# A long convolution's transforms as plain fp32 matmuls of the tiles themselves, in place of three fp32r matmuls of high and low parts

## Chip, core and metric

The kernel runs on one NeuronCore of a Trainium2 chip. The metric is the device time of one execution in microseconds (us), smaller is better. Engines have these names here: PE (TensorE, matmuls), DVE (VectorE), ACT (ScalarE), POOL (GpSimd) and SP (SyncE, which here only issues DMAs; "SPq" is its queue).

## The reference, cut to what matters

The reference is a two-layer diffusion backbone. The second layer's mixer runs a Hyena operator beside differential attention; the change touches only the Hyena operator's two long convolutions, which the reference writes with an FFT:

```
def bidir_fft_conv(u, h_fwd, h_bwd):
    L, C = h_fwd.shape
    k = jnp.concatenate([h_fwd, jnp.zeros((1, C), h_fwd.dtype), h_bwd[1:][::-1]], axis=0)
    uf = jnp.fft.rfft(u.astype(jnp.float32), n=2 * L, axis=1)
    kf = jnp.fft.rfft(k, n=2 * L, axis=0)
    y = jnp.fft.irfft(uf * kf[None], n=2 * L, axis=1)[:, :L]
...
        z = v
        for o, gate in enumerate((x1, x2)):
            z = gate * (bidir_fft_conv(z, h[:, o, 0], h[:, o, 1]) + z * hy_bias[o])
```

Here L is 1024 and C is 512. Everything is float32.

## The kernel before, in words

`hy_conv` holds the two convolutions ("orders", `o` = 0 and 1). The FFT is a matmul with matrices of cosines and sines that come from DRAM. The 1024 rows are taken as four residues `r` (in the order `RS` = 0, 2, 1, 3), a tile `hz` of 128 x 2 x 512 each. For one residue `forward` makes four sums, `fa_ps` (two halves `kt` of the frequencies, `c` = real and imaginary), each the sum of two products of a 128x128 matrix with a 128x512 tile. `take` folds the sums of two residues into tiles `hw` on DVE. When all four residues are there, `spectrum` multiplies by the filter's spectrum `hk`, on DVE alone, `kt` = 0 and then `kt` = 1: 16 operations on 128x1024 and 16 on 128x512 for each `kt`. It leaves one tile for each residue, two in `ht` and two in `hw`. `backward` then makes two sums `y_ps` for each residue, each of four products (two with the tiles of `kt` = 0, two with those of `kt` = 1), and DVE multiplies the sum by the gate, which stands in `hz`. So each order has 32 products forward and 32 backward, 128 in all.

A product is not one matmul. `split` (L91 to L95) makes of each tile a high part in fp32r (a copy on ACT) and a low part (tile minus high part, on DVE), the matrices come from DRAM in two parts already, and `mm3` (L98 to L105) makes three matmuls of each product: high with high (L103), and the two mixed ones (L104, L105). Each is 128x128 with 128x512, in fp32r. The tiles `hz_hi`, `hz_lo` are the parts of `hz`, `hbhi`, `hblo` those of `ht` and `hw`.

The order of the stages around it is this:
- Order 0's forward transforms run among the last steps of the attention (`weave`: scores `s_ps`, transposes `pt_ps`, and the product with the values `o_ps`, L2244, which is one plain fp32 matmul of 128x128 with 128x512; the trace has two records for each).
- Order 0's spectrum runs while the attention ends.
- Order 0's backward and order 1's forward transforms follow each other residue by residue. I call this stretch the middle stage.
- Order 1's spectrum, with the out-projection of the attention's half (`ho_t` transposes, `ho_ps` matmuls by `mm3`, 192 of them) beside it on PE. The generator `proj_half` is advanced by a count, `due += 0.33` for each of the spectrum's steps.
- Order 1's backward transforms, the store of `hy`, and then the MLP's first part, which reads `hy` back (`y_in`) and starts with `op_ps`.

The engines run their instructions in the order of the program text that the scheduler leaves, one queue for each engine. POOL issues the loads of the matrices (`hm`, L1993) and also makes the low parts `wo_lo` of the out-projection's weights, so a load can stand behind a `wo_lo`. SP issues the loads of `hz`, `hk`, `wo_raw` and others.

Of the kernel before, what the change touches and what calls it, by code (L numbers as in the profile page):

```python
# [8 lines left out]
F32 = mybir.dt.float32  # L9
FR = mybir.dt.float32r  # L10
# [1934 lines left out]
def hy_conv(g, pool):  # L1945
# [1 line left out]

    nc = g.nc
    g.hy = g.dram.tile([1024, HY], F32, name="hy")
    RS = (0, 2, 1, 3)
# [35 lines left out]
    def load_mat():  # L1989
        if todo:  # L1990
            src, i, j = todo.pop(0)
            m = pool.tile([128, 2, 2, 2, 128], FR, name="hm", bufs=3)
            nc.gpsimd.dma_start(out=m.rearrange("p a b w k -> p (a b w k)"), in_=g.i[src][i, j])  # L1993
            mats.append(m)

    def matrix():
# [1 line left out]
        return mats.pop(0)  # L1998

    def load_z(j, r):  # L2000
        z = tile2("hz", 2)
        nc.sync.dma_start(out=z, in_=rows(g.hv[j], r))
        return z

    def parts(z, name, bufs):
        hi, lo = (tile2(name + x, bufs, FR) for x in ("hi", "lo"))
        split(g, hi, lo, z)
        return hi, lo

    def forward(r, z, A):  # L2010

        hi, lo = z

        def take(kt, c, ps):
            a = A[kt]
            if r < 2:
                if c == 0:
                    a["d", r] = tile2("hw", 8)
                nc.scalar.copy(a["d", r][:, c], ps)
                return  # L2020
            i = r - 2
            if c == 0:
                a["s", i] = tile2("hw", 8)
            d = a["d", i][:, c]
            add(a["s", i][:, c], ps, d)
            nc.vector.scalar_tensor_tensor(d, ps, -1.0, d, op0=ALU.mult, op1=ALU.add)

        for kt in range(2):
            m = matrix()
            for c in range(2):  # L2030
                ps = psa(g, [128, HY], name="fa_ps", tag="hy")
                mm3(g, ps, [(m[:, c, j, 0], m[:, c, j, 1], hi[:, j], lo[:, j]) for j in range(2)])
                flush()
                later.append(lambda kt=kt, c=c, ps=ps: take(kt, c, ps))
                yield 1
# [59 lines left out]
    def backward(o, r, A, made):  # L2095

        z = load_z(1 + o, r)
        bs = [parts(A[kt][r], "hb", 3) for kt in range(2)]
        yield 1

        def take(jt, ps):
            mul(z[:, jt], ps, z[:, jt])
# [7 lines left out]
        for jt in range(2):  # L2110
            m = matrix()
            ps = psa(g, [128, HY], name="y_ps", tag="hy")
            mm3(g, ps, [(m[:, kt, c, 0], m[:, kt, c, 1], bs[kt][0][:, c], bs[kt][1][:, c])
                        for kt in range(2) for c in range(2)])
            flush()
            later.append(lambda jt=jt, ps=ps: take(jt, ps))
            yield 1
# [1 line left out]
    for _ in range(2):  # L2119
        load_mat()  # L2120
    A = [{}, {}]
    zs = [load_z(0, r) for r in RS[:2]]
    for i, r in enumerate(RS):
        z = parts(zs[i], "hz_", 1)
        if i + 2 < 4:
            zs.append(load_z(0, RS[i + 2]))
        yield 1
        yield from forward(r, z, A)
    flush()
    for o in range(2):  # L2130
        for kt in range(2):
# [2 lines left out]
        for i, r in enumerate(RS):  # L2134
            yield from backward(o, r, A, zs)
            if o == 0:
                if z:
                    yield from forward(RS[i - 1], z, nxt)
                flush()
                z = parts(zs.pop(r), "hz_", 1)  # L2140
        flush()
        if o == 0:
            yield 1
# [250 lines left out]
def tile_kernel(ctx, tc, ins, out):  # L2394
# [93 lines left out]
    with ExitStack() as st:  # L2488
# [14 lines left out]
        with tc.tile_pool(name="ho1", bufs=1, reuse_waits="tile") as pool:  # L2503
# [5 lines left out]
            for n, kind in enumerate(hyena):  # L2509
                if n % 16 == 8:  # L2510
                    next(rest, None)
                due += 0.33 if kind == 2 else 0.0
                if due >= 1.0:
                    next(half, None)
                    due -= 1.0
# [20 lines left out]
def _consts():  # L2536
# [42 lines left out]

    r, kt, p, im, jt, k = np.ix_(*(np.arange(n) for n in (4, 2, 128, 2, 2, 128)))  # L2580
    m = turns(kt * 128 + k, 4 * (jt * 128 + p) + r, im)
    c["k_df"] = np.ascontiguousarray(parts(m)).reshape(4, 2, 128, 1024)

    r, jt, k, kt, im, p = np.ix_(*(np.arange(n) for n in (4, 2, 128, 2, 2, 128)))
    m = turns(kt * 128 + k, 4 * (jt * 128 + p) + r, im) / 1024
    c["k_di"] = np.ascontiguousarray(parts(m)).reshape(4, 2, 128, 1024)

    im, b, kt, x, p, s, k = np.ix_(*(np.arange(n) for n in (2, 2, 2, 2, 128, 4, 128)))
    m = turns(kt * 128 + k + 512 * b, 2 * (s * 128 + p) + x, im)
# [21 lines left out]
```

## Time and profile before

| what | value |
|---|---|
| median of 3 runs | 3460.94 us (3454.71 to 3467.56) |
| the profiled execution | 3455.77 us, its span in the trace 3454.0 us |
| mean granted PE clock in it | 0.954 of full speed |
| busy share of the span | PE 91%, DVE 76%, ACT 45%, POOL 22% |
| the Hyena convolution's stretch of the trace | from about 2433 to 2722 us |

A busy share is the mean over a span of many stages that have different bounds: the 91% of PE says nothing of a stage in which PE waits for DVE. PE's matmuls overlap, so a row's own duration is longer than the step from its start to the next row's start; the step is what a row of many matmuls costs.

### The profile page before, as it was taken

To read this page: it belongs to the slowest core of one execution; us is meant where nothing else is said; L and a number is where in the kernel's file an instruction comes from. 1 tells how busy PE (TensorE), PEld (TensorE's weight loads), DVE (VectorE), ACT (ScalarE), POOL (GpSimd) and SP (SyncE) were. 2 spreads that over 40 slices of the span, in tenths; PEclk is the share of its full clock that TensorE was granted. 3 is DMA by queue.
4 is the path that set the end of the run, shared out by engine and by line. 5 is a ranking of instruction groups with operands and counts; after the bars stand their busy time and mean duration, and the time that the engine had idled before them with its cause. 6 is when DMAs were issued, how large, how long until landed. Compare 5 with 4: busy or idle time off the path is not lost.

```text
span 3454.0 us, 42343 instructions
## 1 busy us (share of the span) xinstructions
PE 3130.1 (91%) x13936; PEld 2437.8 (71%) x13936; DVE 2612.2 (76%) x4530; ACT 1562.4 (45%) x3174; POOL 742.6 (22%) x540
## 2 busy tenths in 40 slices
PE   8888899889987999989998899999848789999998
PEld 4766677567766788878876777776536667887886
DVE  6788998878658776767688665778798589877776
ACT  4444766555555222223345543677532352224443
POOL 0254655523321222101110122100030112210000
PEclk9999999899998999999999999999979899999999
DMA  6544111477753334378777365332445635438954
GB/s 225 151 128 140 49 43 42 135 215 219 256 198 107 131 134 144 130 263 292 234 244 252 104 196 170 103 84 60 139 154 168 224 105 190 140 137 301 316 188 150
DMA packets 346632, 575.10 MB, mean 167 GB/s; under 512 B 43329, under 2 KB 138561, under 8 KB 346284
## 3 DMA queue, kind: packets, MB, share of 16 engines
q1 hardware_dynamic: 296244, 491.17, 43.7%
q10 hardware_dynamic: 40952, 47.67, 4.0%
q0 software_dynamic: 9216, 33.56, 3.5%
q8 instruction: 110, 1.80, 0.2%
q14 instruction: 110, 0.90, 0.1%
HBM read 418.74 MB, written 153.54 MB: 166 GB/s over the span
## 4 chain that ended last, share of the span: by engine, by line
PE 57%; DVE 22%; DMA 7%; issue 6%; ACT 4%; POOL 3%; SPq 0%; ACTq 0%; POOLq 0%; DVEq 0%
PE up_ps L105 5%; PE up_ps L104 5%; PE up_ps L103 5%; PE dn_ps L1527 5%; PE dn_ps L1526 5%; PE dn_ps L1528 5%; DVE gq_lo L95 3%; DVE gq_mx L732 2%; PE s_ps L637 2%; PE o_ps L2244 1%; PE up_ps L1245 1%; DVE ada_acc L261 1%; PE pj_ps L104 1%; PE pj_ps L103 1%; PE pj_ps L105 1%
## 5 line engine op out<-in xcount | busy, mean ns | idle before, releaser
L1526 PE MATMUL dn_ps<-dn_w_hi,dn_h_hi 128*128 128x512 f32 x896 | 352.3, 395 | 30.6 <-DVE accy L1507 17.0
L1527 PE MATMUL dn_ps<-dn_w_lo,dn_h_hi 128*128 128x512 f32 x896 | 353.8, 395 | 4.9 <-DVE dn_w_lo L95 4.7
L1528 PE MATMUL dn_ps<-dn_w_hi,dn_h_lo 128*128 128x512 f32 x896 | 352.6, 394 | 0.0
L95 POOL TENSOR_TENSOR w_lo<-up_w,w_hi 128x512 fp32r<-128x512 f32 x106 | 145.9, 1386 | 579.5 <-ACT w_hi L94 565.5
L94 ACT ACTIVATE dn_h_hi<-dn_h 128x512 fp32r<-128x512 f32 x224 | 140.8, 629 | 278.3 <-PE dn_ps L1527 193.0
L95 DVE TENSOR_TENSOR dn_h_lo<-dn_h,dn_h_hi 128x512 fp32r<-128x512 f32 x224 | 162.6, 726 | 80.4 <-ACT dn_h_hi L94 80.0
L1526 PEld LDWEIGHTS dn_ps<-dn_w_hi,dn_h_hi 128*128 128x128 f32 x896 | 170.4, 190 | 71.2 <-DVE accy L1507 19.0
L765 POOL TENSOR_TENSOR gq_acc<-gq_acc,gq_p 128x512 f32<-128x512 f32 x128 | 183.9, 1437 | 87.4 <-ACT gq_p L754 83.9
L1527 PEld LDWEIGHTS dn_ps<-dn_w_lo,dn_h_hi 128*128 128x128 f32 x896 | 170.5, 190 | 44.1 <-DVE dn_w_lo L95 8.6
L1528 PEld LDWEIGHTS dn_ps<-dn_w_hi,dn_h_lo 128*128 128x128 f32 x896 | 170.4, 190 | 35.3
L95 DVE TENSOR_TENSOR gq_lo<-gq_p,gq_hi 128x512 fp32r<-128x512 f32 x168 | 177.5, 1068 | 20.0 <-ACT gq_hi L94 19.6
L261 DVE SCALAR_TENSOR_TENSOR ada_acc<-w_ada,sc,ada_acc 128x512 f32<-128x512 f32 x224 | 172.7, 808 | 19.9 <-DMA w_ada<-in_w_ada 19.2
L95 POOL TENSOR_TENSOR ada_hl<-ada_acc,ada_hl 128x512 fp32r<-128x512 f32 x32 | 63.9, 2007 | 512.4 <-ACT ada_hl L94 443.0
L94 ACT ACTIVATE s_hi<-up_w 128x512 fp32r<-128x512 f32 x128 | 79.2, 630 | 195.8 <-DVE up_w L1234 122.5
L103 PE MATMUL up_ps<-t_hi,s_hi 128*128 128x512 f32 x384 | 153.0, 398 | 2.0 <-ACT t_hi L94 1.3
L105 PE MATMUL up_ps<-t_hi,s_lo 128*128 128x512 f32 x384 | 152.7, 399 | 2.2 <-DVE s_lo L95 2.2
L1234 DVE TENSOR_TENSOR up_w<-up_w 128x512 f32<-128x512 f32 x128 | 92.3, 724 | 81.4 <-POOL w_lo L95 79.6
L104 PE MATMUL up_ps<-t_lo,s_hi 128*128 128x512 f32 x384 | 152.7, 398 | 1.1 <-DVE t_lo L95 1.1
L647 DVE TENSOR_REDUCE sm_m<-s_ps 128x1 f32<-128x512 f32 (+1 forms) x192 | 110.7, 596 | 43.8 <-PE s_ps L637 42.6
L661 ACT ACTIVATE df_p<-s_ps,sm_m 128x512 f32<-128x512 f32 (+1 forms) x192 | 116.9, 620 | 39.8 <-DVE sm_m L651 37.2
L754 ACT ACTIVATE gq_p<-st_ps 128x512 f32<-128x512 f32 x168 | 99.4, 597 | 73.0 <-PE st_ps L752 55.6
L94 ACT ACTIVATE w_hi<-up_w 128x512 fp32r<-128x512 f32 x106 | 64.6, 628 | 148.4 <-DMA up_w<-in_w_mlp_in 68.3
(512 smaller groups left out, 9198.9 us busy)
## 6 DMA issues: line engine op xcount, KB each, us to landing
dn_b<-in_w_mlp_out SPq DMA_DIRECT2D x252, 256.0 KB
w_ada<-in_w_ada SPq DMA_DIRECT2D x96, 512.0 KB
up_w<-in_w_mlp_in SPq DMA_DIRECT2D x32, 1024.0 KB
hy_m<-in_k_ff POOLq DMA_DIRECT2D x32, 512.0 KB, 5.7
dn_c<-hidc SPq DMA_DIRECT2D x64, 256.0 KB
x<-x_in SPq DMA_DIRECT2D x26, 512.0 KB
x_in<-x SPq DMA_DIRECT2D x26, 512.0 KB
cb_raw<-in_od_w_in SPq DMA_DIRECT2D x20, 512.0 KB
```

The costliest lines, as they stand in the source:

```text
L94: g.nc.scalar.activation(hi, src, ACTF.Copy)
L95: (g.nc.gpsimd if pool else g.nc.vector).tensor_tensor(lo, src, f(hi), op=ALU.subtract)
L103: nc.tensor.matmul(out, ah, bh, start=(i == 0), stop=False)
L104: nc.tensor.matmul(out, ah, bl, start=False, stop=False)
L105: nc.tensor.matmul(out, al, bh, start=False, stop=(i == n - 1))
L261: nc.vector.scalar_tensor_tensor(acc[:, s], w[:, k], sc, acc[:, s], op0=ALU.mult, op1=ALU.add)
L647: nc.vector.tensor_reduce(m[:, i:i + 1], s, axis=AX.X, op=ALU.max)
L661: g.nc.scalar.activation(d, s, ACTF.Exp, bias=m, scale=0.125, accum_out=l[:, i:i + 1])
L765: nc.gpsimd.tensor_tensor(sums[u], sums[u], p, op=ALU.add)
L1526: nc.tensor.matmul(ps, hh[:, sl], wh, start=(k == 0), stop=False)
L1527: nc.tensor.matmul(ps, hh[:, sl], wl, start=False, stop=False)
L1528: nc.tensor.matmul(ps, hl[:, sl], wh, start=False, stop=(k == nb - 1))
```

## The change

The transforms take the tiles and the matrices as they are, in float32, with one matmul for each product in place of three. The splits of `hz` and of the spectrum's results are no longer made, a matrix tile has half its size (256 KB in place of 512 KB), there are four `hm` buffers in place of three and four `hz` buffers in place of two, the four `hz` loads of order 0 stand together ahead of the first transform, the `yield`s that followed the splits are gone, and the out-projection's count is 0.28 in place of 0.33.

```diff
     def load_mat():
         if todo:
             src, i, j = todo.pop(0)
-            m = pool.tile([128, 2, 2, 2, 128], FR, name="hm", bufs=3)
-            nc.gpsimd.dma_start(out=m.rearrange("p a b w k -> p (a b w k)"), in_=g.i[src][i, j])
+            m = pool.tile([128, 2, 2, 128], F32, name="hm", bufs=4)
+            nc.gpsimd.dma_start(out=m.rearrange("p a b k -> p (a b k)"), in_=g.i[src][i, j])
...
     def load_z(j, r):
-        z = tile2("hz", 2)
+        z = tile2("hz", 4)
...
-    def parts(z, name, bufs):
-        hi, lo = (tile2(name + x, bufs, FR) for x in ("hi", "lo"))
-        split(g, hi, lo, z)
-        return hi, lo
+    def products(ps, terms):
+        for i, (m, x) in enumerate(terms):
+            nc.tensor.matmul(ps, m, x, start=(i == 0), stop=(i == len(terms) - 1))
...
-                mm3(g, ps, [(m[:, c, j, 0], m[:, c, j, 1], hi[:, j], lo[:, j]) for j in range(2)])
+                products(ps, [(m[:, c, j], z[:, j]) for j in range(2)])
...
         z = load_z(1 + o, r)
-        bs = [parts(A[kt][r], "hb", 3) for kt in range(2)]
-        yield 1
+        bs = [A[kt][r] for kt in range(2)]
...
-            mm3(g, ps, [(m[:, kt, c, 0], m[:, kt, c, 1], bs[kt][0][:, c], bs[kt][1][:, c])
-                        for kt in range(2) for c in range(2)])
+            products(ps, [(m[:, kt, c], bs[kt][:, c]) for kt in range(2) for c in range(2)])
...
-    zs = [load_z(0, r) for r in RS[:2]]
+    zs = [load_z(0, r) for r in RS]
     for i, r in enumerate(RS):
-        z = parts(zs[i], "hz_", 1)
-        if i + 2 < 4:
-            zs.append(load_z(0, RS[i + 2]))
-        yield 1
-        yield from forward(r, z, A)
+        yield from forward(r, zs[i], A)
...
-                due += 0.33 if kind == 2 else 0.0
+                due += 0.28 if kind == 2 else 0.0
```

Three places show what this does to the engines' queues. A row is an instruction's line, its operation, what it writes and reads, its shape and how often it stands there in a row.

The first place is PE after the attention's last transpose `ot_ps`. Before:

```order
L2257 MATMUL ot_ps<-ident,o_sb 128x128 x4
L1111 MATMUL ho_t<-ident,ho_y 128x128 x8
L103 MATMUL ho_ps<-wo_hi_23393,ho_hi 128x512
L104 MATMUL ho_ps<-wo_lo_23394,ho_hi 128x512
L103 MATMUL y_ps<-hbhi,hm 128x512
L105 MATMUL ho_ps<-wo_hi_23393,ho_lo 128x512
```

And with the change:

```order
L2248 MATMUL ot_ps<-ident,o_sb 128x128 x4
L2006 MATMUL y_ps<-ht,hm 128x512 x4
L2006 MATMUL y_ps<-hw,hm 128x512 x4
L2006 MATMUL y_ps<-ht,hm 128x512 x4
L2006 MATMUL y_ps<-hw,hm 128x512 x4
L2006 MATMUL fa_ps<-hz,hm 128x512 x8
L2006 MATMUL y_ps<-ht,hm 128x512 x8
L2006 MATMUL fa_ps<-hz,hm 128x512 x8
L2006 MATMUL y_ps<-hw,hm 128x512 x8
L2006 MATMUL fa_ps<-hz,hm 128x512 x16
L1111 MATMUL ho_t<-ident,ho_y 128x128 x8
```

The out-projection's transposes stood right behind the attention and ahead of every `y_ps`; with the change all 64 products of the middle stage stand ahead of them, and the first eight (four with `ht`, four with `hw`) read only the tiles of `kt` = 0.

The second place is POOL's queue in the same stretch, after the first eleven loads (eight of `in_k_df`, three of `in_k_di`). Before:

```order
L95 TENSOR_TENSOR wo_lo_23394<-wo_raw,wo_hi_23393 128x1024
L95 TENSOR_TENSOR wo_lo_23400<-wo_raw,wo_hi_23399 128x1024
L95 TENSOR_TENSOR wo_lo_23406<-wo_raw,wo_hi_23405 128x1024
L95 TENSOR_TENSOR wo_lo_23412<-wo_raw,wo_hi_23411 128x1024
L1993 DMA hm<-in_k_di 128x1024
L95 TENSOR_TENSOR wo_lo_23523<-wo_raw,wo_hi_23522 128x1024
L1993 DMA hm<-in_k_df 128x1024
```

With the change, after the first twelve loads:

```order
L1992 DMA hm<-in_k_df 128x512 x2
L95 TENSOR_TENSOR wo_lo_23322<-wo_raw,wo_hi_23321 128x1024
L1992 DMA hm<-in_k_di 128x512
L95 TENSOR_TENSOR wo_lo_23328<-wo_raw,wo_hi_23327 128x1024
L1992 DMA hm<-in_k_di 128x512
L95 TENSOR_TENSOR wo_lo_23334<-wo_raw,wo_hi_23333 128x1024
L1992 DMA hm<-in_k_df 128x512
L95 TENSOR_TENSOR wo_lo_23340<-wo_raw,wo_hi_23339 128x1024
L1992 DMA hm<-in_k_df 128x512
L95 TENSOR_TENSOR wo_lo_23405<-wo_raw,wo_hi_23404 128x1024
```

The first four `wo_lo` stood ahead of the middle stage's loads; now two loads stand ahead of the first `wo_lo`, and the others alternate with single loads.

The third place is PE's order around the first transform of order 0. Before, it stands behind both `cv_ps` groups (the short convolution's transposes) and further attention work; with the change it reads:

```order
L2235 MATMUL o_ps<-pt,dvT 128x512
L2006 MATMUL fa_ps<-hz,hm 128x512 x2
L1688 MATMUL cv_ps<-ident,hy_cv 128x128 x4
L2006 MATMUL fa_ps<-hz,hm 128x512
L1688 MATMUL cv_ps<-ident,hy_cv 128x128 x4
L2006 MATMUL fa_ps<-hz,hm 128x512 x2
```

So the first two products now stand ahead of the last two `cv_ps` groups. At the other end, the last `fa_ps` of order 0 had all the scores ahead of it before; now the last score and 14 steps of the attention (`pt_ps`, `o_ps`) stand behind it, where before it was 10 steps and no score.

## Rows read from the trace of the kernel before

**Rows 1.** Busy time by window: busy us (rows) of each engine, granted clock, DMA

```profile
2440.00:2480.00 40.00, 38.67 (x167) 27.14 (x166) 25.54 (x62) 24.04 (x57) 3.18 (x6) 0.95 0.59 178
```

**Rows 2.** Timeline of PE: start us, us, what, idle before it and releaser

```profile
2432.42 1.02 PE L2244 MATMUL o_ps<-pt,dvT 128*128 128x512 f32 x2
...
2447.74 0.73 PE L103 MATMUL fa_ps<-hz_hi,hm 128*128 128x512 f32 x2 [0.95 <-ACT hz_hi L94]
...
2558.22 1.11 PE L1111 MATMUL ho_t<-ident,ho_y 128*128 128x128 f32 x4 [44.60 <-DMA ho_y<-y1d]
...
2672.83 0.80 PE L104 MATMUL y_ps<-hblo,hm 128*128 128x512 f32 x1 [6.09 <-DVE hblo L95]
...
2673.85 0.63 PE L103 MATMUL y_ps<-hbhi,hm 128*128 128x512 f32 x1
2674.28 0.63 PE L104 MATMUL y_ps<-hblo,hm 128*128 128x512 f32 x1
...
2693.20 0.39 PE L103 MATMUL y_ps<-hbhi,hm 128*128 128x512 f32 x1
...
2699.34 0.39 PE L103 MATMUL y_ps<-hbhi,hm 128*128 128x512 f32 x1
...
2704.35 0.39 PE L105 MATMUL y_ps<-hbhi,hm 128*128 128x512 f32 x1
```

**Rows 3.** The chain of waits, in order of time: start us, us, what

```profile
2455.84 0.44 PE pt_ps L2235 x4
...
2459.78 0.86 PE o_ps L2244 x2
...
2466.55 1.17 PE s_ps L637 x6
...
2722.17 0.80 PE op_ps L103
```

**Rows 4.** `o_ps` alone: ns min/median/max, first and last start

```profile
L2244 PE MATMUL o_ps<-pt,dvT x160: 590/593/1062, 2209.6 to 2511.7; 128*128 128x512 f32 x160
```

**Rows 5.** Groups by shape, 2430 to 2725: busy us, mean ns, idle before

```profile
L95 DVE TENSOR_TENSOR hblo<-ht,hbhi 128x1024 fp32r<-128x1024 f32 x8 | 14.5, 1812 | 2.2 <-ACT hbhi L94 2.2
```

**Rows 6.** Timeline of DVE, order 0's and order 1's spectrum

```profile
2490.82 1.21 DVE L1967 TENSOR_TENSOR ht<-hw 128x1024 f32<-128x1024 f32 x1
...
2511.48 0.16 DVE L116 SCALAR_TENSOR_TENSOR rs_t<-rs_t 128x4 f32<-128x4 f32 x1 [2.13 <-ACT rs_t L115]
...
2545.83 2.31 DVE L116 SCALAR_TENSOR_TENSOR rs_t<-rs_t 128x4 f32<-128x4 f32 x1
...
2549.19 2.31 DVE L117 TENSOR_TENSOR rs_t<-rs_t 128x4 f32<-128x4 f32 x1
...
2562.20 1.28 DVE L95 TENSOR_TENSOR ho_lo<-ho_t,ho_hi 128x512 fp32r<-128x512 f32 x2
...
2618.70 1.21 DVE L1967 TENSOR_TENSOR ht<-hw 128x1024 f32<-128x1024 f32 x1
...
2668.02 1.22 DVE L1973 TENSOR_TENSOR hw<-hw,hk 128x1024 f32<-128x1024 f32 x1
2669.15 0.68 DVE L1970 TENSOR_TENSOR hw<-hw,ht 128x512 f32<-128x512 f32 x1
2669.76 0.68 DVE L1967 TENSOR_TENSOR hw<-hw,ht 128x512 f32<-128x512 f32 x1
...
2675.21 1.23 DVE L1967 TENSOR_TENSOR ht<-hw 128x1024 f32<-128x1024 f32 x1
...
2679.90 1.22 DVE L95 TENSOR_TENSOR hblo<-ht,hbhi 128x1024 fp32r<-128x1024 f32 x1
```

**Rows 7.** Timeline of POOL, the out-projection's low parts

```profile
2545.08 6.40 POOL L95 TENSOR_TENSOR wo_lo<-wo_raw,wo_hi 128x1024 fp32r<-128x1024 f32 x2 [52.72 <-ACT wo_hi L94]
...
2571.33 2.41 POOL L95 TENSOR_TENSOR wo_lo<-wo_raw,wo_hi 128x1024 fp32r<-128x1024 f32 x1
...
2582.11 2.81 POOL L95 TENSOR_TENSOR wo_lo<-wo_raw,wo_hi 128x1024 fp32r<-128x1024 f32 x1
```

More of the change, by code (lines that the diff above doesn't have):

```diff
@@ L2000, in load_z @@
     def load_z(j, r):
-        z = tile2("hz", 2)
+        z = tile2("hz", 4)
         nc.sync.dma_start(out=z, in_=rows(g.hv[j], r))
         return z
-    def parts(z, name, bufs):
-        hi, lo = (tile2(name + x, bufs, FR) for x in ("hi", "lo"))
-        split(g, hi, lo, z)
-        return hi, lo
+    def products(ps, terms):
+        for i, (m, x) in enumerate(terms):
+            nc.tensor.matmul(ps, m, x, start=(i == 0), stop=(i == len(terms) - 1))
     def forward(r, z, A):
-        hi, lo = z
         def take(kt, c, ps):
@@ L2139, in hy_conv @@
                 flush()
-                z = parts(zs.pop(r), "hz_", 1)
+                z = zs.pop(r)
         flush()
@@ L2581, in _consts @@
     m = turns(kt * 128 + k, 4 * (jt * 128 + p) + r, im)
-    c["k_df"] = np.ascontiguousarray(parts(m)).reshape(4, 2, 128, 1024)
+    c["k_df"] = np.ascontiguousarray(m.astype(f4)).reshape(4, 2, 128, 512)
     r, jt, k, kt, im, p = np.ix_(*(np.arange(n) for n in (4, 2, 128, 2, 2, 128)))
     m = turns(kt * 128 + k, 4 * (jt * 128 + p) + r, im) / 1024
-    c["k_di"] = np.ascontiguousarray(parts(m)).reshape(4, 2, 128, 1024)
+    c["k_di"] = np.ascontiguousarray(m.astype(f4)).reshape(4, 2, 128, 512)
     im, b, kt, x, p, s, k = np.ix_(*(np.arange(n) for n in (2, 2, 2, 2, 128, 4, 128)))
```

## The prediction, made before the changed kernel ran

> **What bounds the kernel now.** I read the windows first, to see which engine is full in which stage, then the timelines of PE and DVE, to see who waits at the borders, then the chain of waits for prices. During the last attention stage PE is busy 38.67 of 40 us [rows 1]: there the transforms and the attention share a full PE, and every matmul counts. In the spectrum of order 0 it is the reverse: DVE works from 2490.82 to 2562.20 with hardly a gap, while PE stands idle for 44.60 us up to 2558.22 [rows 2, 6]. The middle stage is PE's again, up to 2618.70, where DVE starts the second spectrum; this lasts to 2679.90 [rows 6]. Then PE finishes order 1's backward transforms at 2704.35, and `op_ps`, the first matmul of the MLP, starts at 2722.17 [rows 2, 3]. So this is a relay: forward on PE, spectrum on DVE, PE, DVE, PE, tail. A time saved at any border moves all that follows. I therefore sum by border.
>
> **What a product costs.** Before, three matmuls: 28 matmuls that read the parts start between 2693.20 and 2699.34 without a wait, 27 steps, 0.227 us each [rows 2], so 0.68 us for a product. After, one plain fp32 matmul. The kernel has this already: `o_ps`, same shape, takes 0.86 us in the chain at full clock [rows 3]. I take 0.86: it is the same operation between other matmuls. Its two records last 593 ns each [rows 4]; if they did not overlap at all in a dense run, a product would take 1.19 us, the upper end. As lower end I keep 0.68, though nothing in the trace makes fp32 as cheap as that. At the half clock (1.2 of 2.4 GHz), as at 2673.85 after a wait, a step is 0.43 us, so everything on PE takes twice as long [rows 2].
>
> The Trainium skill (FP8 and Floating Point Precision, TensorE Precision Notes) speaks against the change: it counts true FP32 as four passes through the array, high with high, both mixed ones and low with low, where the kernel's own split makes three. The rows agree in kind (0.86 against 0.68). Four steps of 0.227 would be 0.91 us, and 112 products on the path would take away 6 us of the gain below.
>
> Each product thus costs 0.18 us more on PE, 128 products 23 us. What is won must come from the borders.
>
> **A. Attention and forward transforms of order 0.** Removed: four splits of `hz`, and the waits for them, such as 0.95 us for `hz_hi` at 2447.74 [rows 2]. Moved: the first products stand ahead of the last `cv_ps`, so they can start when the `o_ps` of 2432.42 ends, at 2433.3 [rows 2, 3], not at 2447.74. Their loads no longer wait for the short convolution. Behind the last product there now stand 14 `o_ps` steps and one score, before 10 and none; PE does them during the spectrum, when it was idle. The order leaves PE this work up to the last score: 32 products (27.4 us), 7 scores of 1.17 (8.2), 7 `o_ps` of 0.86 (6.0), 33 `pt_ps` at 0.44 for four (3.6), 8 `cv_ps` and 4 `ot_ps` at the same price (1.3) [rows 3], together 46.5, and I add 2.5 us for waits. That ends at 2482.3. The spectrum's first row stands ahead of the last score's maxima and of three of the last `take` rows on DVE, about 2.3 us earlier: 2480 against 2490.82. **Gain 10.8 us.** If the attention's own softmax on DVE and ACT, not PE, sets this pace, the gain falls to about 2 us.
>
> **B. Spectrum of order 0.** Its own 16 large operations a half step 1.13 us and the small ones 0.61 [rows 6]; twice 16 of each are 55.6 us. Before it took 71.4 us (2490.82 to 2562.20), so 15.8 us were other things: one `hblo` (1.1), a wait of 2.13 for ACT, and two tiny operations that took 2.31 us each at 2545.83 and 2549.19 where the same kind takes 0.16 at 2511.48 [rows 6]. Beside these two ran a pair of `wo_lo` on POOL from 2545.08, 6.40 us long [rows 7]. After, the order puts all `wo_lo` behind two loads that wait for the middle stage's matmuls, so beside the spectrum there are none. Out go 1.1 + 2.1 + 4.3 us; in come three `take` rows (1.8) and a part of the last score's work. I count 10.8 others: 66.4 us, the end at 2546.4. **Gain 5.0.**
>
> The Trainium skill (SBUF — State Buffer, SBUF: two separate sides) says that GpSimd and DVE operations with two SBUF inputs share one port pair under an exclusive lock, the later one blocked for the whole instruction. The two rows of 2.31 us agree with that. If they had another reason than `wo_lo`, the 4.3 us would stay, and B would gain 0.7.
>
> **C. Middle stage.** Before: 56.5 us from 2562.20 to 2618.70. After, all 64 products stand ahead of the out-projection. Eight read only tiles of `kt` = 0 and run while PE has nothing else. The tile that the next ones need is written one large and four small operations before the spectrum's end, 3.5 us, as at 2675.21 plus one step in the other spectrum [rows 6]. So PE starts at 2542.9 with 56 products, 48.0 us. I add 2.5 us for the half clock after the idle time, three products' worth. Then there is POOL. Loads alternate with `wo_lo`, whose starts are 3.6 us apart (four between 2571.33 and 2582.11 [rows 7]); eight take 29 us from about 2547, and by my bookkeeping loads come late by 3, 4 and 4 us, partly the same lateness: I take 5, with 0 and 20 as ends. The last product ends at 2598.4. The second spectrum starts ahead of the last three takes, 2 us earlier, at 2596.4. So 50.0 us against 56.5: **gain 6.5**, from the splits that no longer stand between DVE's tiles and PE and from the out-projection's matmuls, which move into the next spectrum, where PE has room.
>
> **D. Spectrum of order 1.** 61.2 us before (2618.70 to 2679.90): 55.6, seven `ho_lo` (4.2) and one `hblo`. After: 55.6, the same `ho_lo`, three takes: 61.6, to 2658.0. **Loss 0.4.**
>
> **E. Backward transforms of order 1.** Before 24.7 us from 2679.90 to the last product's end at 2704.6. There PE waits for `hblo` (6.09 us at 2672.83 [rows 2] still beside the spectrum), whose eight rows on `ht` average 1812 ns in this stretch [rows 5]. After, no split: the tile that 24 products wait for is written 3.5 us before the spectrum's end, as above; 20.6 us and again 2.5 for the half clock, from 2654.5 on, make 2677.6, so 19.6 us. **Gain 5.1.** With four `hz` buffers all gates are there in time.
>
> **F. Tail.** 17.8 us from the last product to `op_ps`, through the store and the next loads. The slower count leaves 60 `ho_ps` behind the last product (24 before), 13.7 us at 0.227, still inside. Were they longer than the tail, each would cost 0.23. Nothing.
>
> **Sum.** 10.8 + 5.0 + 6.5 − 0.4 + 5.1 = 27.0 us, `op_ps` at 2695.2. Nothing behind it changes. All of it was priced at bare steps, so I give back 1 us for hand-overs. The profiled execution took 3455.8 us, 5.2 less than the median 3460.9; 26 us less than the median are **3435 us**. What a measurement of this kernel can tell from no change is about 0.5%, 17 us: faster means below 3443.6, slower above 3478.2.
>
> **The rivals.**
> - *POOL's queue sets the middle stage.* Loads behind `wo_lo` are late by 20 us, not 5. For it: the alternation in the order. Against it: a load is needed only every four products (3.4 us), four buffers. Then 3450, no measurable change.
> - *The attention sets its own pace.* A gains 2: 3444, on the border. For it: DVE and ACT are busy 25.54 and 24.04 of 40 us there, and scores are handed over through them. Against it: PE is at 38.67 [rows 1].
> - *Only PE counts, and this ends slower.* If in A, C and E PE has work enough anyway, and the waits for splits are merely re-labelled as waits for tiles, then no border moves earlier and the fourth pass alone is left: 128 × 0.18 = 23 us, 3484. It decides from 17 us on, that is if less than 6 us of the borders' gain comes. For it: the 91% of PE. Against it: the 44.60 us idle, and a `kt` = 0 half that can run in them.
> - *The fp32 product is dearer in a dense run.* At 1.19 us the 112 products on the path lose 37 us: 3472, no measurable change; it needs 1.25 us to be slower.
>
> **How the numbers follow.** The sum as it stands, with costs within their ends: 0.60, 3420 to 3446. POOL's queue 0.14, attention's pace 0.11, dear product 0.07, only PE 0.08. Faster: the 0.60 less a little at its upper edge, half of the attention's case, and partial mixtures of it: 0.70. Slower: the case of PE alone and a dear product at the half clock: 0.09. The rest, 0.21, is the same. Leaving out the worst of POOL and the dear cases above 3455 and below 3414, the range is 3414 to 3455.
>
> **What would show it.** Right: a product's step in dense runs 0.85 to 0.87; the first `fa_ps` near 2433; spectrum starts near 2480 and 2596; no 2.31 us rows in the first spectrum; `op_ps` near 2695. Wrong: waits of PE for `hm` of more than 5 us in the middle stage (POOL); waits of PE for scores' results before the spectrum (attention); steps over 0.9 at full clock (product); a half clock through the middle stage, which would add 0.86 us a product.

## The result, and the profile after

The changed kernel takes 3424.24 us in the median of four runs (3421.57 to 3426.17), the kernel before 3462.05 us beside it. The ratio is 0.9887, 95% interval 0.9866 to 0.9908: 1.1% faster, about 38 us. Forecast were 3435 us and a range from 3414 to 3455. The profiled execution took 3425.51 us, with a span of 3423.7 us.

First PE, in the timeline of the changed kernel (the answers to [rows 2]). The columns are start, length, instruction, and the idle time before it with what ended it. Rows of one kind are merged here; a product has two records, so x16 are eight products.

```profile
2433.88 0.40 PE L1668 MATMUL hc_ps<-ftx_hi,cb_lo 128*128 128x512 f32 x1
...
2438.90 1.88 PE L2006 MATMUL fa_ps<-hz,hm 128*128 128x512 f32 x4
...
2484.64 1.18 PE L637 MATMUL s_ps<-dkT,dqT 128*128 128x512 f32 x4
...
2519.52 5.56 PE L2006 MATMUL y_ps<-ht,hm 128*128 128x512 f32 x8 [5.12 <-DVE ht L1966]
2524.91 3.60 PE L2006 MATMUL y_ps<-hw,hm 128*128 128x512 f32 x8
2543.01 5.76 PE L2006 MATMUL y_ps<-ht,hm 128*128 128x512 f32 x8 [14.50 <-DVE ht L1966]
2548.61 3.60 PE L2006 MATMUL y_ps<-hw,hm 128*128 128x512 f32 x8
...
2558.91 7.03 PE L2006 MATMUL y_ps<-ht,hm 128*128 128x512 f32 x16
2565.77 7.03 PE L2006 MATMUL fa_ps<-hz,hm 128*128 128x512 f32 x16
2573.94 3.67 PE L2006 MATMUL y_ps<-hw,hm 128*128 128x512 f32 x8 [1.14 <-DMA hm<-in_k_di]
2578.82 3.67 PE L2006 MATMUL y_ps<-hw,hm 128*128 128x512 f32 x8 [1.21 <-DMA hm<-in_k_di]
2582.33 13.90 PE L2006 MATMUL fa_ps<-hz,hm 128*128 128x512 f32 x32
2596.06 1.04 PE L1111 MATMUL ho_t<-ident,ho_y 128*128 128x128 f32 x8
...
2668.64 7.03 PE L2006 MATMUL y_ps<-hw,hm 128*128 128x512 f32 x16
...
2696.05 0.79 PE L103 MATMUL op_ps<-wo_hi,y_hi 128*128 128x512 f32 x1 [3.42 <-ACT y_hi L94]
```

Eight products with the tiles of `kt` = 0 now run at 2519.52 and 2524.91, in what was PE's long idle time. All of the middle stage stands ahead of `ho_t` at 2596.06. From 2558.91 to 2565.77 eight products take 6.86 us: 0.858 us each in a dense run, as `o_ps` had shown alone [rows 3]. Two waits for `hm` are left, 1.14 and 1.21 us.

Next DVE, in the timeline of the same run (the answers to [rows 6]).

```profile
2482.42 1.22 DVE L1966 TENSOR_TENSOR ht<-hw 128x1024 f32<-128x1024 f32 x1
...
2541.62 0.15 DVE L116 SCALAR_TENSOR_TENSOR rs_t<-rs_t 128x4 f32<-128x4 f32 x1
2541.73 1.23 DVE L1966 TENSOR_TENSOR ht<-hw 128x1024 f32<-128x1024 f32 x1
2542.88 0.15 DVE L117 TENSOR_TENSOR rs_t<-rs_t 128x4 f32<-128x4 f32 x1
...
2547.62 0.68 DVE L1972 TENSOR_TENSOR hz<-y_ps,hz 128x512 f32<-128x512 f32 x1
...
2594.23 1.22 DVE L1966 TENSOR_TENSOR ht<-hw 128x1024 f32<-128x1024 f32 x1
...
2651.97 1.23 DVE L1966 TENSOR_TENSOR ht<-hw 128x1024 f32<-128x1024 f32 x1
...
2656.83 0.69 DVE L1972 TENSOR_TENSOR hz<-y_ps,hz 128x512 f32<-128x512 f32 x1
```

The spectra start at 2482.42 and 2594.23. The two tiny operations that took 2.31 us now take 0.15 us. The tile for which PE waits is written by the row at 2541.73, and PE starts at 2543.01. Then POOL, in the timeline of the same run (the answer to [rows 7]):

```profile
2547.09 0.54 POOL L1992 DMA_DIRECT2D hm<-in_k_df  x1 [63.10 <-PE y_ps L2006]
2549.07 0.54 POOL L1992 DMA_DIRECT2D hm<-in_k_df  x1 [1.44 <-PE y_ps L2006]
2549.62 2.36 POOL L95 TENSOR_TENSOR wo_lo<-wo_raw,wo_hi 128x1024 fp32r<-128x1024 f32 x1
```

Two loads wait up to 2549.07 for the middle stage's products, and only behind them comes the first `wo_lo`, after the spectrum's end.

To compare all runs I cut the stretch at four borders that the timelines give: the last `hc_ps` (the short convolution's input, at 2428.26 before and 2433.88 after), the first row of each spectrum, the end of the last `y_ps`, and the first `op_ps`. The times are differences of starts in the profiled executions, in us; for the last `y_ps` it is the end of its row.

| kernel | hc_ps to spectrum 0 | to spectrum 1 | to the last y_ps | to op_ps | sum | median of the runs |
|---|---|---|---|---|---|---|
| before | 62.6 | 127.9 | 86.0 | 17.4 | 293.9 | 3462.1 |
| forecast for the change | 51.7 | 116.4 | 81.2 | 17.6 | 266.9 | 3435 |
| after | 48.5 | 111.8 | 81.4 | 20.4 | 262.2 | 3424.2 |
| before_again | 61.4 | 130.4 | 86.4 | 17.5 | 295.6 | 3462.7 |
| changed_again | 48.5 | 111.1 | 81.7 | 20.8 | 262.1 | 3423.0 |
| splits_kept | 54.5 | 113.0 | 83.0 | 20.4 | 270.9 | 3438.1 |
| products_twice | 68.7 | 162.8 | 110.1 | 20.4 | 361.9 | 3525.2 |
| three_matmuls | 60.9 | 120.9 | 85.8 | 20.4 | 287.9 | 3452.3 |
| room_taken | 55.7 | 110.4 | 81.8 | 20.4 | 268.3 | 3432.1 |
| yields_back | 50.3 | 126.8 | 81.1 | 21.0 | 279.1 | 3442.3 |
| forward_fp32_only | 54.1 | 117.1 | 90.2 | 22.2 | 283.5 | 3447.4 |
| backward_fp32_only | 59.7 | 112.6 | 79.3 | 21.2 | 272.7 | 3432.9 |
| count_040 | 48.5 | 111.3 | 86.4 | 8.6 | 254.9 | 3418.0 |
| count_045 | 48.5 | 110.3 | 86.0 | 8.1 | 252.9 | 3416.9 |
| count_045_low_on_dve | 48.5 | 110.0 | 86.2 | 8.1 | 252.7 | 3412.6 |

The stretch is 31.7 us shorter than in the first profile of before, 33.4 than in the second. The kernel before ran beside three groups of kernels, on its own medians of 3462.3, 3458.7 and 3462.9 us, so medians of different groups compare to some 4 us only; within a group they share it. Outside of the stretch (span less stretch) the fourteen profiles run from 3152.6 to 3167.5 us.

### The profile page after: what moved, and what is told of

Its sections match the earlier page's. It is cut to its first block, busy times and chain, and to the rows that moved or that the text cites. A ratio compares the mean times of both kernels' runs of the same rounds, so it can differ in the third digit from the quotient of the medians.

```text
span 3423.7 us, 42030 instructions
## 1 busy us (share of the span) xinstructions
PE 3129.8 (91%) x13808; PEld 2402.8 (70%) x13808; DVE 2570.6 (75%) x4506; ACT 1538.5 (45%) x3150; POOL 736.5 (22%) x540
## 4 chain that ended last, share of the span: by engine, by line
PE 56%; DVE 21%; issue 8%; DMA 7%; ACT 4%; POOL 3%; SPq 0%; ACTq 0%; POOLq 0%; DVEq 0%
PE up_ps L105 5%; PE up_ps L104 5%; PE up_ps L103 5%; PE dn_ps L1527 5%; PE dn_ps L1526 5%; PE dn_ps L1528 5%; DVE gq_lo L95 2%; DVE gq_mx L732 2%; PE s_ps L637 2%; PE up_ps L1245 1%; PE o_ps L2235 1%; DVE ada_acc L261 1%; DMA dn_b<-in_w_mlp_out 1%; PE pj_ps L104 1%; PE pj_ps L103 1%
## 5 line engine op out<-in xcount | busy, mean ns | idle before, releaser
L1526 PE MATMUL dn_ps<-dn_w_hi,dn_h_hi 128*128 128x512 f32 x896 | 352.9, 396 | 30.4 <-DVE accy L1507 16.1
L95 DVE TENSOR_TENSOR dn_h_lo<-dn_h,dn_h_hi 128x512 fp32r<-128x512 f32 x224 | 161.7, 722 | 79.7 <-ACT dn_h_hi L94 79.3
L94 ACT ACTIVATE s_hi<-up_w 128x512 fp32r<-128x512 f32 x128 | 79.3, 630 | 190.4 <-DVE up_w L1234 116.3
```

Source lines behind the costliest of these rows:

```text
L94: g.nc.scalar.activation(hi, src, ACTF.Copy)
L95: (g.nc.gpsimd if pool else g.nc.vector).tensor_tensor(lo, src, f(hi), op=ALU.subtract)
L1526: nc.tensor.matmul(ps, hh[:, sl], wh, start=(k == 0), stop=False)
```

## The experiments

### What repeats

`before_again` is the kernel before, word for word, and `changed_again` the changed one.

> The kernel before, unchanged, profiled and timed a second time. The profiled stretch from the last short-convolution matmul hc_ps (2428.3 before, 2433.9 after) to the first op_ps (2722.17 and 2696.05) was 293.9 us before and 262.2 us after, a gain of 31.7 us, while the medians differ by 37.8 us. Theory A (the whole gain lies in the convolution; the rest is scatter of the kernel's other stages): the ratio to before is 1.000, its median lies some us above its first profiled 3455.8, the same stretch is again 293 to 295 us, and the parts outside of it differ from the first profile by several us either way. Theory B (the change also speeds or slows stages outside): the parts outside of the stretch repeat to 1 us here, so the 5.6 us by which the changed kernel came late to the stretch and the 4.2 us by which it was faster behind it are the change's.

Measured: ratio 1.000 (0.999 to 1.001), 3462.66 us. The stretch is 295.6 us. Outside of the stretch the two profiles of before differ by 5.1 us (span 3454.0 less 293.9 is 3160.1; 3460.8 less 295.6 is 3165.2), where nothing was changed. So the theory that all lies in the convolution stands, as far as a profile can tell: 3161.5 us outside of the stretch with the change lie between the two. The two long rows of tiny operations are there again (timeline of DVE in `before_again`):

```profile
2547.60 2.31 DVE L116 SCALAR_TENSOR_TENSOR rs_t<-rs_t 128x4 f32<-128x4 f32 x1
...
2550.97 2.30 DVE L117 TENSOR_TENSOR rs_t<-rs_t 128x4 f32<-128x4 f32 x1
```

> The changed kernel once more, beside the next three on the same chip. Its profile again shows which parts of the stretch repeat: first spectrum 48 to 49 us behind the last hc_ps, second spectrum 111 to 113 us behind the first, last y_ps 81 to 82 us behind that, 20 us to op_ps. Ratio to before 0.987 to 0.990.

Measured: 0.9886 (0.9869 to 0.9904), 3423.0 us. The borders repeat to 0.7 us.

### The arithmetic undone, the order kept: `three_matmuls`

```diff
-            products(ps, [(m[:, kt, c], bs[kt][:, c]) for kt in range(2) for c in range(2)])
+            mm3(g, ps, [(m[:, kt, c, 0], m[:, kt, c, 1], bs[kt][0][:, c], bs[kt][1][:, c])
+                        for kt in range(2) for c in range(2)])
...
-        bs = [A[kt][r] for kt in range(2)]
+        bs = [parts(A[kt][r], "hb", 2) for kt in range(2)]
```

and the same for the forward transforms.

> The changed kernel, with only the arithmetic undone: splits and three fp32r matmuls for each product, matrices in two parts (three buffers of 512 KB), two buffers in place of three for the spectra's parts; four hz buffers and loads up front, no yields behind the splits, and the count of 0.28 stay as changed. Theory relay with the order (of some 32 us, about a third comes from what stands where: the out-projection's transposes behind the middle stage, early loads): 3440 to 3452, between the two kernels. Rival (all of it is the arithmetic): 3458 to 3465. Rival (all of it is the order and the buffers; three cheap matmuls are as good): 3418 to 3430.

Measured: 0.9975 (0.9963 to 0.9987), 3452.3 us, 0.3 us above the first theory's range. With the old arithmetic, the new order and buffers gain 6.0 to 7.7 us in the stretch, nearly all of it between the two spectra, less 3 us that the tail gives back. Both rivals fall: it is neither only the arithmetic nor only the order.

### One direction at a time: `forward_fp32_only` and `backward_fp32_only`

Both are `three_matmuls` with one direction's `mm3` and splits replaced by `products`, and with a matrix tile of its own for each direction.

> The changed kernel with the backward transforms as before (split results of the spectrum, three fp32r matmuls, di matrices in two parts and three buffers of their own, two buffers for the parts), the forward transforms in plain fp32. Theory relay: stage A as in room_taken (the first loads wait for the short convolution, 3429 to 3434 alone), and in the middle stage and at the end the waits for hblo return, about half of the 9 and 4 us that these two stages gained over three_matmuls: 3436 to 3444, between the changed kernel (3424) and three_matmuls (3452). Rival (only the forward transforms count, since they had the splits in front of a full PE): within 3 us of room_taken.

> The changed kernel with the forward transforms as before (split tiles, three fp32r matmuls, matrices in two parts) and the backward ones in plain fp32. Theory relay with room: the first loads wait for the short convolution and stage A is as in three_matmuls (first spectrum 61 us behind hc_ps, 48.5 with the change), the last transforms as with the change (81 us, 86 in three_matmuls), the middle stage between (116, 112 and 121): 3434 to 3442. Rival (the last transforms gained nothing from the arithmetic): 3444 to 3452.

Measured: 0.9967 (0.9955 to 0.9979), 3447.4 us, and 0.9914 (0.9894 to 0.9934), 3432.9 us. Against `three_matmuls` the forward transforms in fp32 give 4.4 us of the stretch (287.9 to 283.5), the backward ones 15.2 us (287.9 to 272.7). The expectation for the first was too low by 3 us, since I had given the backward transforms too little; for the second it was too high by 1 us. Why the backward ones weigh more is seen in PE's timeline of `forward_fp32_only` behind the last spectrum, where the waits for splits are back, and two for matrices that are twice as large again:

```profile
2661.02 0.79 PE L104 MATMUL y_ps<-hblo,hm 128*128 128x512 f32 x1 [5.18 <-DVE hblo L95]
...
2666.87 0.51 PE L103 MATMUL y_ps<-hbhi,hm 128*128 128x512 f32 x1 [0.92 <-ACT hbhi L94]
2668.10 0.50 PE L104 MATMUL y_ps<-hblo,hm 128*128 128x512 f32 x1 [0.72 <-DVE hblo L95]
...
2673.08 0.50 PE L104 MATMUL y_ps<-hblo,hm 128*128 128x512 f32 x1 [0.76 <-DVE hblo L95]
...
2677.99 0.47 PE L103 MATMUL y_ps<-hbhi,hm 128*128 128x512 f32 x1 [0.72 <-DMA hm<-in_k_di]
2679.88 0.47 PE L103 MATMUL y_ps<-hbhi,hm 128*128 128x512 f32 x1 [1.41 <-DMA hm<-in_k_di]
...
2688.03 0.50 PE L104 MATMUL y_ps<-hblo,hm 128*128 128x512 f32 x1 [0.76 <-DVE hblo L95]
```

and in the waits of `backward_fp32_only` between 2540 and 2600, where it is the forward transforms' splits (total us, times, longest):

```profile
PE fa_ps L104 <- DVE hz_lo L95: 4.0, 2, 3.1
PE fa_ps L103 <- ACT hz_hi L94: 1.6, 1, 1.6
```

The longest of these is more than a split's own length. The low part that PE waits for stands beside POOL's `wo_lo` (timelines of PE, DVE and POOL in `backward_fp32_only`):

```profile
2559.04 0.50 PE L104 MATMUL fa_ps<-hz_lo,hm 128*128 128x512 f32 x1 [3.11 <-DVE hz_lo L95]
...
2554.16 4.82 DVE L95 TENSOR_TENSOR hz_lo<-hz,hz_hi 128x1024 fp32r<-128x1024 f32 x1
...
2555.53 2.36 POOL L95 TENSOR_TENSOR wo_lo<-wo_raw,wo_hi 128x1024 fp32r<-128x1024 f32 x1
```

It takes 4.82 us, where others take 1.22, and ends at 2558.98, 1.09 us behind the `wo_lo`. So a part of what a split costs in the middle stage comes from the `wo_lo` beside it. The old arithmetic with the `wo_lo` off POOL was not run, and neither was a kernel with the smaller matrices alone, so how much of the 19.6 us each of them is stays open.

### The splits made, but read by nobody: `splits_kept`

```diff
         bs = [A[kt][r] for kt in range(2)]
+        for x in bs:
+            parts(x, "hb", 2)
...
+        parts(zs[i], "hz_", 1)
         yield from forward(r, zs[i], A)
...
                 z = zs.pop(r)
+                parts(z, "hz_", 1)
```

> The changed kernel, with the 24 splits of hz, ht and hw made as before on ACT and DVE (a high and a low part each), but read by nobody: the matmuls take the fp32 tiles. So DVE and ACT have their old work, and PE waits for none of it. Theory relay (what counted was that the splits stood between an engine's result and the next engine's start): most of the gain stays; DVE has 24 rows of about 1.2 us more, of which two or three stand inside the spectra and up to two ahead of the last gate multiplications: 3 to 10 us, 3427 to 3434. Rival (what counted was DVE's time, 38 us of low parts less): nearly all of the gain is gone, 3450 to 3462.

Measured: 0.9931 (0.9912 to 0.9950), 3438.1 us, outside both ranges. The rival (DVE's time) falls: DVE made all 24 low parts again, and most of the gain stayed. But the stretch is 8.7 us longer than after, and 6.0 of these lie ahead of the first spectrum, where four splits among PE's full work should have cost nothing. In the program's order the first loads of `hm` and `hz` wait for the short convolution's `hy_cv` here, as before. That led to the next kernel.

### Only the room: `room_taken`

```diff
     zs = [load_z(0, r) for r in RS]
+    pads = [pool.tile([128, 2, HY], FR, name=f"pad{i}") for i in range(6)]
...
+    for x in pads:
+        nc.scalar.copy(x[:, 0, 0:2], g.ident[:, 0:2])
```

> The changed kernel with 24 KB per partition of its SBUF taken by six tiles that nobody reads (each gets two columns from ACT between the forward transforms and the first spectrum). No split is made. In the order this gives the first matrix and gate loads the same waits for the short convolution (hy_cv) as in the kernel before, and the first fa_ps again stands behind both cv_ps groups. Theory room (much of what stage A gained is not the splits' time but the SBUF that their tiles no longer take, so the first loads need not wait for the short convolution's buffers): first fa_ps about 15 us behind the last hc_ps (19.5 before, 5.0 after), the first spectrum 54 us behind it (62.6 before, 48.5 after), 3429 to 3434. Rival (stage A gained by the splits that are no longer made): first spectrum at 49 us behind hc_ps, 3423 to 3427.

Measured: 0.9926 (0.9904 to 0.9948), 3432.1 us. The stretch is 6.1 us longer than after. The timeline of PE in this kernel, from the short convolution's transposes to the first transform:

```profile
2435.01 0.63 PE L1688 MATMUL cv_ps<-ident,hy_cv 128*128 128x128 f32 x4 [1.41 <-DVE hy_cv L1710]
...
2445.33 5.32 PE L2006 MATMUL fa_ps<-hz,hm 128*128 128x512 f32 x12
```

The first `fa_ps` starts 16.9 us behind the last `hc_ps` (2428.44); after, it was 5.0 us (2433.88 to 2438.90). No split is made, so this is the room alone. The matrix loads show it, in POOL's timelines of `room_taken` and of the changed kernel:

```profile
2435.42 1.59 POOL L1992 DMA_DIRECT2D hm<-in_k_df  x3 [66.02 <-DVE hy_cv L1710]
```

```profile
2434.61 1.60 POOL L1992 DMA_DIRECT2D hm<-in_k_df  x3 [31.85 <-PE hc_ps L1668]
```

They go out 7.0 us behind the last `hc_ps` (0.7 after). So 24 KB per partition, the size of the parts' tiles in `splits_kept`, decide whether the first loads have a place before the short convolution gives its own free. Of the 14.1 us that the first stage gained, 7.2 are this (55.7 less 48.5). `splits_kept` costs 2.6 us beyond it (270.9 less 268.3): that is what 24 splits cost on ACT and DVE when nobody waits for them. The four times of `room_taken` spread over 17 us (3424.7 to 3441.4), and the profiled execution is the shortest, so its evidence is the stretch, not the median.

### Only the yields: `yields_back`

```diff
         bs = [A[kt][r] for kt in range(2)]
+        yield 1
...
     for i, r in enumerate(RS):
+        yield 1
         yield from forward(r, zs[i], A)
```

> The changed kernel with only the yields back where the splits were. By the order the out-projection's eight transposes and twelve of its matmuls stand ahead of nearly all y_ps of the middle stage again, four wo_lo stand ahead of the middle stage's loads on POOL, and the scores come a few rows later between the forward transforms. Theory relay with the order: the early half of eight products waits behind ho_t, so the middle stage is 5 to 8 us longer, and a pair of wo_lo beside the first spectrum brings back two DVE rows of 2.3 us in place of 0.15 us: 3432 to 3440. Rival (the order counts for nothing, PE catches up): 3422 to 3428.

Measured: 0.9956 (0.9941 to 0.9971), 3442.3 us, 2 us above the range; the rival (no effect) falls. The stretch is 16.9 us longer than after, 15.0 of it from spectrum to spectrum, which is then as long as before the change (126.8; 127.9 before). The timeline of PE shows the place:

```profile
2544.47 1.97 PE L1111 MATMUL ho_t<-ident,ho_y 128*128 128x128 f32 x8 [42.86 <-DMA ho_y<-y1d]
...
2550.64 1.72 PE L2006 MATMUL y_ps<-ht,hm 128*128 128x512 f32 x2
...
2554.21 5.31 PE L2006 MATMUL y_ps<-ht,hm 128*128 128x512 f32 x12
```

PE stands 42.86 us before an out-projection transpose whose input's DMA is late, and the eight early products stand behind it. Behind the idle time the granted clock is 0.50 (2544 to 2552), and the first `y_ps` starts at 2550.64; with the change those eight were done at 2528.5. DVE and POOL, in the timelines of this kernel:

```profile
2532.49 2.31 DVE L116 SCALAR_TENSOR_TENSOR rs_t<-rs_t 128x4 f32<-128x4 f32 x1
...
2535.86 2.30 DVE L117 TENSOR_TENSOR rs_t<-rs_t 128x4 f32<-128x4 f32 x1
```

```profile
2531.74 6.40 POOL L95 TENSOR_TENSOR wo_lo<-wo_raw,wo_hi 128x1024 fp32r<-128x1024 f32 x2 [48.79 <-ACT wo_hi L94]
```

A pair of `wo_lo` is beside the first spectrum again, and so are the two rows of 2.3 us. The 15.0 us have two parts. From the spectrum's first row to the row that writes the tile for PE it is 64.1 us (2478.83 to 2542.92) in place of 59.3: 4.8 us, of which the two rows make 4.3. The other 10.2 us lie behind: eight products (6.9 us) that no longer run early, and the eight transposes and twelve `ho_ps` among them, in part at half the clock.

### Every product twice: `products_twice`

```diff
-        for i, (m, x) in enumerate(terms):
-            nc.tensor.matmul(ps, m, x, start=(i == 0), stop=(i == len(terms) - 1))
+        for _ in range(2):
+            for i, (m, x) in enumerate(terms):
+                nc.tensor.matmul(ps, m, x, start=(i == 0), stop=(i == len(terms) - 1))
```

> The changed kernel, with each of the sums on PE made twice into the same bank, the second in place of the first: 256 plain fp32 products in place of 128, 0.86 us each. Theory relay (PE's products are on the path in the forward transforms of order 0, the middle stage and the end, 112 of them, and hidden behind the spectrum for the eight plus eight that are made early): 112 x 0.86 = 96 us more, less some 3 us of waits for matrices that now come in time: 3510 to 3520. Rival (PE has room, only DVE's chain counts): under 40 us, below 3464. The price of a product in a dense run would show as 0.86 us a step again.

Measured: 1.0186 (1.0163 to 1.0209), 3525.2 us, 5 us above the range. The stretch is 99.7 us longer than after. The rival (PE has room) falls. That my 112 products of 0.858 us make 96, so near, is luck: only eight products run early in each spectrum here too, not sixteen, so all 128 second copies, 110 us, come on top of what stood on the path. By stage the stretch grows by 20.2, 51.0 and 28.7 us for 32, 64 and 32 products, which is 0.63, 0.80 and 0.90 us for each: nearly a product's length in the two later stages, three quarters of it among the attention.

### The out-projection's count: `count_040`, `count_045`, `count_045_low_on_dve`

```diff
-                due += 0.28 if kind == 2 else 0.0
+                due += 0.40 if kind == 2 else 0.0
```

> The changed kernel with the out-projection's count at 0.40 in place of 0.28: no ho_ps is left behind the last transform (60 with 0.28), 20 stand between the last spectrum's end and the last transforms. Theory (the tail from the last y_ps to op_ps took 20.4 us in place of 17.4 because ACT's copies of ho_ps stand ahead of the MLP's w_hi on ACT): the tail is 17 us again, the last spectrum is as long, 3 us less: 3420 to 3422. Rival (the MLP needs the same weights whenever; what the tail gains the rest of op_ps loses): 3423 to 3426. Rival (out-projection matmuls inside the last spectrum or the transforms delay y_ps): 3426 to 3432.

> The changed kernel with the count at 0.45: all 192 ho_ps stand ahead of the 32 last products, none between or behind them. With 0.40 the tail fell from 20.4 to 8.6 us, but 20 ho_ps stood between the last spectrum's early products and the rest, and the last transforms ended 5 us later. Theory (those 20 matmuls at 0.23 us delayed them): the tail stays at 9 us, the last products end 81 to 83 us behind the spectrum's start as with 0.28: 3412 to 3415. Rival (PE has not the room for all of the out-projection beside the spectrum, 47 us of it in 58): 3418 to 3424.

> As count_045, with the eight wo_lo of the out-projection's weights on DVE in place of POOL, where in the order they stand among the gate multiplications and takes of the middle stage, in which DVE waits for PE most of the time. POOL then only issues loads there. Theory relay: what POOL's wo_lo cost are the two waits for hm in the middle stage, 1.14 and 1.21 us in the changed kernel, so 2 us less than count_045, if DVE's takes are not late. Rival (POOL's queue holds up more than the waits show): 5 us or more less. Rival (DVE's rows of 1.2 us delay the takes): 1 to 4 us more.

Measured: 0.9883 (0.9866 to 0.9899), 3418.0 us, 2 us below its range; 0.9867 (0.9847 to 0.9887), 3416.9 us, between the ranges of theory and rival; 0.9857 (0.9838 to 0.9877), 3412.6 us. In the last group `changed_again` took 3423.0 us (3419.7 to 3425.7) and `count_045` 3416.9 (3414.6 to 3418.2), 6 us less, with the stretch 9.2 us shorter: faster than both kernels. The tail falls from 20.4 to 8 us, far more than I expected. In the changed kernel SP, which loads `y_in`, had to wait for one of the last `ho_ps` (waits of SP's queue, 2660 to 2700, and below it the same wait before the change, 2690 to 2725):

```profile
SPq L1149 <- PE ho_ps L105: 8.4, 1, 8.4
```

```profile
SPq L1149 <- PE ho_ps L104: 0.5, 1, 0.5
```

The timeline of PE in `count_045`:

```profile
2670.56 7.03 PE L2006 MATMUL y_ps<-hw,hm 128*128 128x512 f32 x16
2683.89 1.94 PE L1155 MATMUL tr_ps<-ident,y_in 128*128 128x128 f32 x8 [6.30 <-DMA y_in<-hy]
2685.72 0.79 PE L103 MATMUL op_ps<-wo_hi,y_hi 128*128 128x512 f32 x1
```

Now the store and reload of `hy` alone stand before `op_ps`. But the stretch to the last `y_ps` is 86.0 us in place of 81.4, with no `ho_ps` between the products, so my theory on the 20 matmuls of `count_040` fell. It is the spectrum itself that is longer: its last big tile is written 62.4 us behind its start (2653.95 less 2591.56; 57.7 with the change), and DVE has a wait that the changed kernel hasn't:

```profile
2606.97 0.69 DVE L95 TENSOR_TENSOR ho_lo<-ho_t,ho_hi 128x512 fp32r<-128x512 f32 x1 [3.73 <-ACT ho_hi L94]
```

It stands in order for a low part of the out-projection. ACT makes the high part 14.8 us behind the spectrum's start in both kernels (2606.34 and 2609.00), but the low part stands earlier in DVE's queue here: 15.4 us behind the start, where the changed kernel has it 17.5 us behind (2611.72) and without a wait. In `count_045_low_on_dve`

```diff
-            half = proj_half(g, w, range(4, KT), range(NC_T, NT), lambda t: y1d[t], pool, True, 0, keep)
+            half = proj_half(g, w, range(4, KT), range(NC_T, NT), lambda t: y1d[t], pool, False, 0, keep)
...
-            rest = wo_rest(g, w, range(4), keep, True, 0)
+            rest = wo_rest(g, w, range(4), keep, False, 0)
```

no wait for `hm` is left in the middle stage, but the stretch is the same to 0.2 us. Its median is 4 us lower, where I expected 2; the intervals overlap, and the profile shows no place for it.

## Why the prediction was right

The direction, the range and the mechanism held: a relay in which each border moves what follows. By its steps, measured from border to border:

- **The price of a product** (0.86) was right: 0.858 in a dense run. The rival of a dearer product fell. The Trainium skill (FP8 and Floating Point Precision, TensorE Precision Notes) counts four passes; by that rule, with the 0.227 us of [rows 2] for a step, an estimate is 0.91 us, and the dense run is below it, so the product is a little cheaper than this estimate.
- **A** (gain 10.8) was too small: 14.1, or 12.9 against the second profile of before. PE's work was right: from the first transform at 2438.90 to the end of the last score, four matmuls of 0.23 us from 2484.64 on, it is 46.7 us, where I summed 46.5; the 2.5 us for waits did not come, and the spectrum starts 3.1 us ahead of that end, not 2.3. What I had not told apart is what to thank. I named the four splits and the loads together; `room_taken` shows that half is the room in SBUF. The rival (the attention sets its own pace) fell.
- **B** (66.4 us) was right: 65.2, to the first gate multiplication at 2547.62. That the rows of 2.31 us go with the `wo_lo` beside them is now shown three times: there in both profiles of before and in `yields_back`, absent after. `products_twice`, with one `wo_lo` beside the spectrum, has one such row, of 2.30 us. What happens is seen in the ends (before, timelines of POOL and of DVE):

```profile
2548.09 3.40 POOL L95 TENSOR_TENSOR wo_lo<-wo_raw,wo_hi 128x1024 fp32r<-128x1024 f32 x1
...
2574.53 2.56 POOL L95 TENSOR_TENSOR wo_lo<-wo_raw,wo_hi 128x1024 fp32r<-128x1024 f32 x1 [0.29 <-ACT wo_hi L94]
...
2575.43 2.75 DVE L95 TENSOR_TENSOR hblo<-ht,hbhi 128x1024 fp32r<-128x1024 f32 x1
```

The second `wo_lo` of the pair starts at 2548.09 and ends at 2551.49; the two rows of 2.31 us [rows 6] end at 2548.14 and 2551.50, each with the `wo_lo` beside it. The low part at 2575.43 ends 1.09 us behind its `wo_lo`, which is about its own length. So a row stands still until the `wo_lo` is done, and then runs. In the middle stage before the change six of the eight `hblo` rows took 1.90 to 3.40 us that way, in place of 1.21; PE had `ho_ps` to do meanwhile and shows no wait for them there. Rows that read one of PE's sums are not held: the changed kernel's middle stage has only such rows, and beside a `wo_lo` they take 0.69 us as alone. The Trainium skill (SBUF — State Buffer, SBUF: two separate sides) gives the reason, one port pair under a lock that the first holds for its whole instruction, for DVE rows with two SBUF inputs; these ends agree with it.

- **C** (50.0 us) was too long: 46.6. The tile is ready 4.7 us before the spectrum's end, not 3.5, since the attention's normalisation stands behind it; and POOL cost 2.35 us, not 5. The rival (POOL's queue) fell, and `count_045_low_on_dve` gains nothing in the stretch without it. I gave two reasons, the splits and the out-projection's matmuls, without their shares. From spectrum to spectrum (B and C) the gain is 16.1 to 18.6 us; with the yields back 1.1 to 3.6 of it are left, with the old arithmetic in the new order 7.0 to 9.5. It takes both: the products must read the tiles directly, and the transposes must not stand ahead of them.
- **D and E** (81.2 together) were right: 81.4. With the splits back it is 85.8 (`three_matmuls`) and 90.2 (`forward_fp32_only`). One reading for E was wrong: the 1812 ns of [rows 5] is a mean over both orders. Behind the last spectrum a low part takes 1.22 or 1.23 us; the long ones are those beside a `wo_lo` in the middle stage.
- **F** (nothing) was the one step that failed: the tail is 3.0 us longer. I held 13.7 us of `ho_ps` against 17.8 us of tail, and did not see that SP's load of `y_in` waits for one of the last of them (8.4 us, 0.5 before).
- **Only PE counts** fell: the kernel is faster. `products_twice` shows what is true in it: from now on each further product costs most of its length.

By parts the stretch adds up: order and buffers with the old arithmetic 6.0 to 7.7 us, forward 4.4, backward 15.2 (together 268.3, as `room_taken` has it), room 6.1. That it fits to 0.1 us is luck. Stage by stage the parts give 52.9, 108.8, 83.7 and 23.0 us, where `room_taken` has 55.7, 110.4, 81.8 and 20.4, so they hold to some 3 us only. The sum of the steps was 27.0 us, the measured stretch 31.7 to 33.4. Against the first profile of before A, B and C gave 3.3, 1.2 and 3.4 us more than I summed and F took 3.0 away, so a part of the misses cancelled. The medians differ by 38 us; the 4 to 6 us between lie outside of the stretch, where two profiles of one kernel differ as much, and I could not place them. I had also taken the forecast from a profiled execution of 3455.8 us and moved it to the median by 5.2 us, which assumes that the scatter of before would be the changed kernel's too.

## What to carry to other kernels

Where engines hand over to each other, count the steps between one engine's result and the next one's start, not each engine's busy time: 24 low parts on DVE cost 2.6 us when nobody waited for them, and a pass more on PE was repaid by starting earlier. Look at who stands at the head of the in-order queue when an engine idles: one transpose that waits for a DMA kept eight ready products behind it, and with the matmuls that came ahead with it this cost the middle stage 10 us. When a row is longer than its kind, look at which engine's row ends with it: the low parts of 2.8 us were rows of 1.2 us that stood for POOL. And a tile that is no longer needed gives back room, too: whether the next stage's first loads have a place before the last stage's buffers are free can be read from the waits of the loads, and tried with a dummy tile.

## What the runs showed of the hardware

- A plain fp32 matmul of 128x128 with 128x512 takes 0.858 us in a dense run (granted clock 1.00 from 2549 to 2596 in the changed kernel), an fp32r one 0.227: one fp32 costs as much as 3.8 fp32r, against the three of the split.
- A DVE row with two inputs in SBUF that meets a running `wo_lo` on POOL stands until it ends: rows of 0.15 us become 2.31, low parts of 1.21 become 1.6 to 4.8 (before, `splits_kept` and the kernels with the old arithmetic). It holds the other way, too: the second `wo_lo` of the pair took 3.40 us behind a DVE row that had begun at 2548.06, just ahead of it, where a `wo_lo` took 2.36 in the changed kernel's middle stage. In the thirteen profiles with `wo_lo` on POOL 75 DVE rows that read one of PE's sums began beside one, and none was longer than its kind.
